# Summing the MLP's closing products in SBUF before the gate, in a four-layer diffusion trunk on one core

## The chip, the cores and the metric
The kernel runs on one core of one Trainium2 chip. The metric is the device time of one execution in microseconds; shown is the median of three runs.

## The reference, cut to what matters
Four layers (differential attention, neighbourhood attention, grouped-query attention, Hyena convolution) work on 128 context and 512 latent tokens of width 1024, all in float32. Each ends in a squared-ReLU MLP of width 4096, whose result is multiplied by a gate (one vector for the context tokens, one for the latent tokens) and added to a scaled residual before a layer norm:

```python
def squared_relu_mlp(h, w1, w2):
    return jnp.square(jax.nn.relu(h @ w1)) @ w2
...
        fp = squared_relu_mlp(modulate(xp, mod_p[3], mod_p[4]), mlp_w1[i], mlp_w2[i])
        fs = squared_relu_mlp(modulate(xs, mod_s[3], mod_s[4]), mlp_w1[i], mlp_w2[i])
        xp = layer_norm(DN_ALPHA * xp + mod_p[5] * fp, ln_g[i, 1], ln_b[i, 1])
        xs = layer_norm(DN_ALPHA * xs + mod_s[5] * fs, ln_g[i, 1], ln_b[i, 1])
```

## The kernel before, in words
The 640 tokens are five tiles of 128 (NT = 5); tile 0 is context. Every large product is made of three matmuls (mm3, L471 to L475), since each float32 operand is split into a rounded high part and a rest. Weights come in units of 512 KB: a load into one of three `raw` buffers (L421), a high part made by ACT (L450) and a rest by DVE (L451), in a fixed order of use (weight_order, L345). All loads and stores are issued by the queue of SP, in order.

The MLP (L865) goes in eight chunks of 512 of the 4096 columns. In a pass `ch` of the loop at L910 the first product of chunk `ch` is made (w1_unit, four units, L918), squared into `ff` by ACT (L875 to L877) with a rest by DVE (L878), and then the closing product of chunk `ch - 1`: 4 quarters q of 256 columns times 5 token tiles, so 20 groups of 12 matmuls, each into one of four one-bank PSUM tiles (any1). The last chunk's closing product is made by sublayer_end, beside the layer norm. The pass of ch = 0 makes only the first product.

After each group, residual (L647) empties the PSUM tile. DVE multiplies it by the gate into `gtmp` (L653), and then `gtmp` is added to the residual `r` (L660). One in four of these adds goes to DVE and three to POOL in layers 0 to 2 (`share` is QM = 1); in layer 3 all go to DVE (QL = 4). The gates come from DRAM as four tiles of 128x512, broadcast to all partitions (load_gates, L607), loaded after the pass of ch = 0; the four tiles of the layer norm's factors are loaded in the pass of ch = 6 (L917). Both sets stay until the end of the sublayer.

Between the units stands side work (side, L539). In layers 0 to 2 that is the modulation of the next layer: 48 steps, each with two 256 KB loads (`adaw`, L431) that DVE multiplies into an accumulator (L541); after every eight steps, four matmuls of PE (L546) read the accumulator. Layer 0 also makes the filter taps of the Hyena layer (L1584 to L1591), layers 1 and 2 their transforms. None of it falls into the pass of ch = 7.

Small tiles of at most 2560 bytes per partition come from one pool of general buffers, `S` (L314), NS = 16 of them: `adaw`, gates, layer-norm factors, `fx` of the MLP, the taps' tiles, and in the mixers the softmax tiles `e`, their transposes `pt`, the queries and keys.

The framework orders the instructions of each engine by a planner that follows the program's order as priority and hands out the buffers of a pool; only POOL, and PE in some stretches, keep the program's order as written. All waits are semaphores that the framework places.

Of the kernel before, what the change touches and what calls it, by code (L numbers as in the profile page):

```python
# [10 lines left out]
F32 = mybir.dt.float32  # L11
# [7 lines left out]
P = 128  # L19
D = 1024  # L20
# [4 lines left out]
NT = TOK // P  # L25
# [253 lines left out]
class Trunk:  # L279
    HL = HLN  # L280
    RAW = RAWN
    NS = 16

    def __init__(self, ctx, tc, a, outs, layers):
        self.ctx, self.tc, self.nc, self.a, self.o, self.layers = ctx, tc, tc.nc, a, outs, layers
# [28 lines left out]
    def S(self, dt, name, n=640):  # L314
        self.tn += 1
        return self.base.tile([P, n], dt, tag="S", bufs=self.NS, name=f"{name}{self.tn}")

# [491 lines left out]
    def quarter(self, u, x, t, q, quick=False):  # L809

        c = slice(t * P, (t + 1) * P)
        ps = self.any1([P, 256], "w2")
        for k in range(4):
            f = slice(k * 256, (k + 1) * 256)
            self.mm3(ps, (x[:, 0, k, c], x[:, 1, k, c]), (u[:, 0, f], u[:, 1, f]), k == 0, k == 3)
        self.residual(ps, t, q, quick)

    def out_half(self):
        self.tn += 1
# [45 lines left out]
    def mlp(self, l, nxt, last):  # L865
        nc = self.nc
        self.share = QL if last else QM
        ff = {}
        groups = 0

        def evac(dst, src):

            w = src.shape[2]
            x = self.S(F32, "fx", src.shape[1] * w).rearrange("p (a b) -> p a b", b=w)
            nc.scalar.activation(x, src, AF.Relu)  # L875
            nc.scalar.activation(x, x, AF.Square)
            nc.scalar.copy(dst[0], x)  # L877
            nc.vector.tensor_sub(dst[1], x, dst[0].bitcast(F32))  # L878

        def run(gen):  # L880
            for _ in gen:
                pass

        def w1_unit(u):
            t = self.wget(("w1", l, u))
            ps = self.b2([P, 2, 512], "w1")
            for half in range(2):
                run(self.span_a(ps[:, half, :HALF], t, half * HALF, half * HALF + HALF))
            evac([ff[u // 4][:, i, u % 4].rearrange("p (a b) -> p a b", a=2) for i in range(2)], ps[:, :, :HALF])

        def w1_first():

            ts = []
            for c0, c1 in ((0, 256), (256, TOK)):
                for pair in range(2):
                    ps = self.b2([P, 2, 512], "w1")
                    for i in range(2):
                        u = 2 * pair + i
                        if c0 == 0:
                            ts.append(self.wget(("w1", l, u), ahead=1))  # L900
                        run(self.span_a(ps[:, i, :c1 - c0], ts[u], c0, c1))
                        if c0 == 0:
                            self.flush(1)
                        else:
                            evac([ff[0][:, n, u:u + 1, c0:c1] for n in range(2)], ps[:, i:i + 1, :c1 - c0])
                    if c0 == 0:
                        evac([ff[0][:, n, 2 * pair:2 * pair + 2, c0:c1] for n in range(2)], ps[:, :, :c1 - c0])
            self.settle()

        for ch in range(8):  # L910
            ff[ch] = self.L(F32R, f"ff{ch}").rearrange("p (a f t) -> p a f t", a=2, f=4)
            if ch == 0:
                w1_first()
                self.load_gates(l, 1)
                continue
            if ch == 6:
                self.load_ln(l, 1, last)  # L917
            for f in range(4):  # L918
                w1_unit(4 * ch + f)
                self.side()  # L920
            for q in range(4):
                u = self.wget(("w2", l, 4 * (ch - 1) + q))
                for t in range(NT):
                    self.quarter(u, ff[ch - 1], t, q)
                    groups += 1
                    if self.taps and groups % TSTEP == 0:
                        self.tap_step()
                self.side()
        while self.taps:
            self.tap_step()  # L930
        self.sublayer_end(l, 1, lambda q, ahead: self.wget(("w2", l, 28 + q), ahead), lambda u, t, q, quick: self.quarter(u, ff[7], t, q, quick), last, nxt in (1, 3), nxt in (1, 2))
# [1140 lines left out]
class GqUnit(PairUnit):  # L2072
    n, chunk, cols, quick = 5, 1, FULL, 2
# [14 lines left out]
class NaUnit(PairUnit):  # L2088
    START = (0, 64, 192, 256)
    CHUNK = (1, 6, 7, 3)  # L2090
    n, quick = 3, 2
# [138 lines left out]
```

## Time and profile before

| | us |
|---|---|
| median of three runs | 3402.54 (3398.75 to 3402.73) |
| the profiled execution | 3399.52 |
| its span, first to last instruction | 3397.7 |

The profile shows one execution. Its rows give an engine's busy time (us), the number of instructions (x) and, for groups of instructions, the mean duration (ns) and how long the engine was idle just before them, with the instruction whose end released it. Windows are us from the start of the span. The four MLPs lie at about 411 to 921, 1244 to 1745, 2062 to 2555 and 2928 to 3383 us.

### The profile page before, as it was taken

What the parts mean: (1) busy time and instruction counts of PE and PEld (TensorE: products, weight loads), DVE (VectorE), ACT (ScalarE), POOL (GpSimd) and SP (SyncE); (2) the same over time, 40 slices, a digit from 0 to 9 for tenths busy, and PEclk for the clock granted to TensorE, in tenths of its full rate; (3) what the DMA queues carried; (4) which work ended last, traced back from release to release, by engine and by line L of the source; (5) the groups of instructions that cost most, each with busy time, mean ns of one, the idle gap of its engine ahead of it and who ended that gap; (6) DMA issues with size and microseconds to landing.
All of it is one profiled execution on the core that took longest, in us unless ns stands there. A gap on an engine that the chain in (4) does not pass through costs nothing.

```text
span 3397.7 us, 63734 instructions
## 1 busy us (share of the span) xinstructions
PE 3288.2 (97%) x25288; PEld 3162.0 (93%) x25288; DVE 2514.5 (74%) x4892; ACT 1526.1 (45%) x2752; POOL 677.2 (20%) x746
## 2 busy tenths in 40 slices
PE   8999999999999999999998999999998999999998
PEld 6888999998999899999997889999998998999998
DVE  4777878887766687787678888877859888855557
ACT  3667643333456564334345655333325334532322
POOL 0000123343323321222222020322321112200002
PEclk9999999999999999999999999999999999999999
DMA  8454245454343426556321123555523224322221
GB/s 285 144 156 128 72 142 178 170 167 160 94 147 103 120 69 205 174 168 211 124 78 50 32 66 117 164 175 179 175 77 126 76 97 153 106 79 75 87 75 51
DMA packets 162763, 429.45 MB, mean 126 GB/s; under 512 B 20574, under 2 KB 30438, under 8 KB 159390
## 3 DMA queue, kind: packets, MB, share of 16 engines
q1 hardware_dynamic: 162464, 425.37, 38.7%
q8 instruction: 199, 3.26, 0.4%
q14 instruction: 100, 0.82, 0.1%
HBM read 371.20 MB, written 34.05 MB: 119 GB/s over the span
## 4 chain that ended last, share of the span: by engine, by line
PE 54%; DVE 13%; issue 4%; ACT 2%; DMA 2%; POOL 2%; SPq 0%; DVEq 0%; POOLq 0%; ACTq 0%
PE w L473 13%; PE w L474 13%; PE w L475 13%; DVE hl L451 2%; PE pv L2057 1%; DVE gtmp L653 1%; DVE ada L541 1%; PE s L2010 1%; PE ptp L1060 1%; PE qk L473 1%; DMA adaw<-in_ada_w 1%; PE qk L475 1%; PE qk L474 1%; PE py L1773 1%; DVE r L660 1%
## 5 line engine op out<-in xcount | busy, mean ns | idle before, releaser
L451 DVE TENSOR_TENSOR hl<-raw,hl 128x1024 fp32r<-128x1024 f32 x411 | 535.1, 1305 | 338.1 <-ACT hl L450 336.8
L450 ACT CAST hl<-raw 128x1024 fp32r<-128x1024 f32 x411 | 430.3, 1048 | 677.0 <-PE w L475 558.8
L660 POOL TENSOR_TENSOR r<-r,gtmp 128x256 f32<-128x256 f32 x416 | 413.9, 1008 | 1564.2 <-DVE gtmp L653 1515.6
L473 PE MATMUL w<-hl,ff 128*128 128x256 f32 x2560 | 715.7, 280 | 7.3 <-DVE gtmp L653 7.0
L474 PE MATMUL w<-hl,ff 128*128 128x256 f32 x2560 | 715.2, 279 | 2.5 <-DVE hl L451 2.4
L475 PE MATMUL w<-hl,ff 128*128 128x256 f32 x2560 | 714.0, 279 | 0.0
L473 PE MATMUL w<-hh,hl 128*128 128x320 f32 (+2 forms) x2048 | 635.7, 310 | 3.8 <-ACT fx L875 3.1
L474 PE MATMUL w<-hl,hl 128*128 128x320 f32 (+2 forms) x2048 | 632.1, 309 | 3.4 <-DVE hl L742 3.3
L475 PE MATMUL w<-hh,hl 128*128 128x320 f32 (+2 forms) x2048 | 632.1, 309 | 0.0
L473 PEld LDWEIGHTS w<-hl,ff 128*128 128x128 f32 x2560 | 481.1, 188 | 11.9 <-DVE gtmp L653 10.1
L474 PEld LDWEIGHTS w<-hl,ff 128*128 128x128 f32 x2560 | 481.2, 188 | 5.0 <-DVE hl L451 3.3
L475 PEld LDWEIGHTS w<-hl,ff 128*128 128x128 f32 x2560 | 480.0, 188 | 0.0
L653 DVE TENSOR_TENSOR gtmp<-w,gate 128x256 f32<-128x256 f32 x800 | 326.6, 416 | 182.6 <-PE w L475 165.9
L541 DVE SCALAR_TENSOR_TENSOR ada<-adaw,sil,ada 128x512 f32<-128x512 f32 x504 | 388.0, 801 | 88.9 <-DMA adaw<-in_ada_w 85.4
L473 PEld LDWEIGHTS w<-hh,hl 128*128 128x128 f32 x2048 | 384.3, 188 | 18.9 <-issue 9.2
L474 PEld LDWEIGHTS w<-hl,hl 128*128 128x128 f32 x2048 | 384.2, 188 | 4.5 <-DVE hl L742 4.1
L475 PEld LDWEIGHTS w<-hh,hl 128*128 128x128 f32 x2048 | 384.1, 188 | 0.8 <-issue 0.8
L875 ACT ACTIVATE fx<-w 128x640 f32<-128x640 f32 (+2 forms) x136 | 91.5, 673 | 462.6 <-PE w L475 444.9
L473 PE MATMUL qk<-hh,hl 128*128 128x320 f32 (+2 forms) x672 | 215.1, 320 | 0.2
L474 PE MATMUL qk<-hl,hl 128*128 128x320 f32 (+2 forms) x672 | 210.6, 313 | 1.7 <-DVE hl L742 1.7
L475 PE MATMUL qk<-hh,hl 128*128 128x320 f32 (+2 forms) x672 | 210.2, 313 | 0.0
L473 PE MATMUL w<-hl,oh 128*128 128x256 f32 x640 | 183.9, 288 | 7.9 <-DVE gtmp L653 5.5
(338 smaller groups left out, 6630.6 us busy)
## 6 DMA issues: line engine op xcount, KB each, us to landing
raw<-in_w SPq DMA_DIRECT2D x256, 512.0 KB
adaw<-in_ada_w SPq DMA_DIRECT2D x288, 256.0 KB
adaw<-in_ada_w SPq DMA_DIRECT2D x16, 1024.0 KB
raw<-ab_d SPq DMA_DIRECT2D x32, 512.0 KB
raw<-in_hy_in SPq DMA_DIRECT2D x24, 512.0 KB
ks<-ks SPq DMA_DIRECT2D x64, 160.0 KB
adaw<-in_ada_s SPq DMA_DIRECT2D x8, 1024.0 KB
raw<-in_da_qk SPq DMA_DIRECT2D x16, 512.0 KB
```

Source lines behind the costliest of these rows:

```text
L450: self.nc.scalar.copy(t[:, 0], raw)
L451: self.nc.vector.tensor_sub(t[:, 1], raw, t[:, 0].bitcast(F32))
L473: mm(ps, w[0], x[0], start=start, stop=False)
L474: mm(ps, w[0], x[1], start=False, stop=False)
L475: mm(ps, w[1], x[0], start=False, stop=stop)
L541: nc.vector.scalar_tensor_tensor(out=y, in0=raw[h], scalar=x, in1=y, op0=ALU.mult, op1=ALU.add)
L653: nc.vector.tensor_mul(tmp, ps, self.gate[2 * s + q // 2][:, (q % 2) * 256:(q % 2) * 256 + 256])
L660: eng.tensor_add(rv, rv, tmp)
L875: nc.scalar.activation(x, src, AF.Relu)
L1060: nc.tensor.transpose(ps[:, i * P:(i + 1) * P], pr[:, (done + i) * P:(done + i + 1) * P], self.ident)
L1773: mm(py[ct][:, par], yh[:, i, cc], inv[h][:, kt, s, par], start=kt == 0 and i == 0 and h == 0, stop=False)
L2010: mm(ps[dst], hd["qs"][h][:, self.qs], ks[:, c], start=n == 0, stop=n == 1)
```

## The change
The closing products of chunks 0 to 5 no longer go through the gate one by one. Their 20 groups per chunk are summed in a new SBUF tile `sums` (128 x 5 x 1024, 20 KB per partition): chunk 0's groups are copied there by ACT, those of chunks 1 to 5 added by DVE, straight from PSUM. In the pass of ch = 7, beside the first product of that chunk, ten pairs of DVE instructions of 128x512 multiply `sums` by the gate and add it to `r`. Chunks 6 and 7 go as before. The gates are loaded in the pass of ch = 6 rather than after ch = 0. To make room, the general buffers go from 16 to 14 and the space kept for descriptors of software-made DMAs is cut to 1024 bytes.

```diff
-    NS = 16
+    NS = 14
...
         ps = self.any1([P, 256], "w2")
+        self.product(ps, u, x, t)
+        self.residual(ps, t, q, quick)
+
+    def product(self, ps, u, x, t):
+        c = slice(t * P, (t + 1) * P)
         for k in range(4):
             f = slice(k * 256, (k + 1) * 256)
             self.mm3(ps, (x[:, 0, k, c], x[:, 1, k, c]), (u[:, 0, f], u[:, 1, f]), k == 0, k == 3)
-        self.residual(ps, t, q, quick)
...
+        sums = self.scr.tile([P, NT, D], F32, tag="sums", bufs=1, name=f"sums{l}")
+
+        def collect(ps, t, c0, first):
+
+            v = sums[:, t, c0:c0 + ps.shape[1]]
+            if first:
+                nc.scalar.copy(v, ps)
+            else:
+                nc.vector.tensor_add(v, v, ps)
+
+        def gated(t, h):
+
+            c = slice(h * 512, (h + 1) * 512)
+            nc.vector.tensor_mul(sums[:, t, c], sums[:, t, c], self.gate[(0 if t == 0 else 2) + h])
+            nc.vector.tensor_add(self.r[:, t, c], self.r[:, t, c], sums[:, t, c])
...
             if ch == 0:
                 w1_first()
+                continue
+            if ch == 6:
                 self.load_gates(l, 1)
-                continue
             if ch == 6:
                 self.load_ln(l, 1, last)
             for f in range(4):
                 w1_unit(4 * ch + f)
+                if ch == 7:
+                    for i in range(f * 10 // 4, (f + 1) * 10 // 4):
+                        gated(i // 2, i % 2)
                 self.side()
             for q in range(4):
                 u = self.wget(("w2", l, 4 * (ch - 1) + q))
                 for t in range(NT):
-                    self.quarter(u, ff[ch - 1], t, q)
+                    if ch == 7:
+                        self.quarter(u, ff[6], t, q)
+                    else:
+                        ps = self.any1([P, 256], "w2")
+                        self.product(ps, u, ff[ch - 1], t)
+                        collect(ps, t, q * 256, ch == 1)
...
-    nc = bacc.Bacc("TRN2", target_bir_lowering=False, num_devices=1)
+    nc = bacc.Bacc("TRN2", target_bir_lowering=False, num_devices=1, dynamic_dma_scratch_size=1024)
```

## Rows read from the trace of the kernel before

**Rows 1.** The page, part 1: busy us of each engine over the span.
```profile
PE 3288.2 (97%) x25288; PEld 3162.0 (93%) x25288; DVE 2514.5 (74%) x4892; ACT 1526.1 (45%) x2752; POOL 677.2 (20%) x746
```

**Rows 2.** Windows, the four MLPs: PE, PEld, DVE, ACT, POOL busy; PEclk, DMA share, GB/s.
```profile
411.00:921.00 510.00, 496.00 (x3637) 474.20 (x3635) 401.91 (x681) 206.17 (x298) 163.36 (x159) 1.00 0.46 151
1244.00:1745.00 501.00, 496.02 (x3796) 486.64 (x3795) 378.29 (x598) 198.84 (x277) 122.47 (x118) 1.00 0.48 160
2062.00:2555.00 493.00, 488.69 (x3751) 479.89 (x3750) 371.94 (x593) 191.15 (x264) 128.08 (x118) 1.00 0.46 152
2928.00:3383.00 455.00, 453.39 (x3478) 452.27 (x3477) 261.11 (x476) 141.97 (x191) 18.89 (x14) 1.00 0.24 76
```

**Rows 3.** Waits of PE, MLP of layer 0 (411 to 921): total us, times, longest.
```profile
PE ada L546 <- DVE ada L541: 5.6, 6, 1.4
PE w L473 <- DVE gtmp L653: 3.8, 3, 1.5
PE filt L1581 <- DVE hab L1573: 2.0, 1, 2.0
...
PE ada L546 <- DVE gtmp L653: 0.2, 1, 0.2
```

**Rows 4.** Waits of PE, MLP of layer 1 (1244 to 1745).
```profile
PE w L474 <- DVE hl L451: 2.4, 2, 1.3
PE w L473 <- DVE gtmp L653: 0.9, 2, 0.6
```

**Rows 5.** Waits of PE, MLP of layer 2 (2062 to 2555).
```profile
PE w L473 <- DVE gtmp L653: 2.4, 4, 1.0
```

**Rows 6.** Groups of instructions, whole span: busy us, mean ns, idle before.
```profile
L660 POOL TENSOR_TENSOR r<-r,gtmp 128x256 f32<-128x256 f32 x416 | 413.9, 1008 | 1564.2 <-DVE gtmp L653 1515.6 <-DVE m L2015 27.4 <-DVE mv L691 15.2
L541 DVE SCALAR_TENSOR_TENSOR ada<-adaw,sil,ada 128x512 f32<-128x512 f32 x504 | 388.0, 801 | 88.9 <-DMA adaw<-in_ada_w 85.4 <-ACT ada L539 3.4
...
L653 DVE TENSOR_TENSOR gtmp<-w,gate 128x256 f32<-128x256 f32 x800 | 326.6, 416 | 182.6 <-PE w L475 165.9 <-POOL r L660 12.8 <-DMA gate<-gate_d 2.0
...
L660 DVE TENSOR_TENSOR r<-r,gtmp 128x256 f32<-128x256 f32 x364 | 167.0, 462 | 7.6
...
L749 DVE TENSOR_TENSOR r<-r,ln_b 128x512 f32<-128x512 f32 x70 | 45.6, 685 | 0.0
L748 DVE TENSOR_TENSOR r<-r,ln_g 128x512 f32<-128x512 f32 x70 | 45.5, 685 | 0.0
...
L952 ACT COPY vv<-v 128x256 f32<-128x256 f32 x40 | 14.7, 370 | 30.5 <-PE v L475 30.3
```

**Rows 7.** Tile ada, layer 0's MLP, 470 to 836: duration ns min/median/max.
```profile
L541 DVE SCALAR_TENSOR_TENSOR ada<-adaw,sil,ada x153: 730/745/1226, 471.4 to 833.6; 128x512 f32<-128x512 f32 x153
```

**Rows 8.** Timeline near 550 us, of DVE and of POOL: start us, us.
```profile
550.52 2.04 DVE L541 SCALAR_TENSOR_TENSOR ada<-adaw,sil,ada 128x512 f32<-128x512 f32 x2
...
549.67 3.49 POOL L660 TENSOR_TENSOR r<-r,gtmp 128x256 f32<-128x256 f32 x3
```

**Rows 9.** Windows, layer 0: pass ch = 6, then first product of ch = 7; neighbourhood attention.
```profile
781.00:836.00 55.00, 51.16 (x373) 46.93 (x372) 52.54 (x84) 22.07 (x31) 24.02 (x23) 1.00 0.51 176
836.00:863.00 27.00, 27.00 (x186) 27.00 (x187) 6.85 (x7) 9.31 (x13) 0.00 (x0) 1.00 0.25 79
965.00:1160.00 195.00, 194.51 (x1569) 186.13 (x1568) 114.71 (x319) 120.14 (x322) 61.49 (x136) 1.00 0.37 105
```

**Rows 10.** Groups of instructions, pass ch = 6 of layer 0 (781 to 836).
```profile
L541 DVE SCALAR_TENSOR_TENSOR ada<-adaw,sil,ada 128x512 f32<-128x512 f32 x28 | 21.6, 803 | 1.2 <-DMA adaw<-in_ada_w 1.2
```

**Rows 11.** Waits of DVE, whole span: total us, times, longest.
```profile
DVE ada L541 <- DMA adaw<-in_ada_w: 85.4, 29, 7.5
```

**Rows 12.** DMA issues, pass ch = 6 of layer 0 (781 to 836).
```profile
adaw<-in_ada_w SPq DMA_DIRECT2D x10, 256.0 KB
```

**Rows 13.** Windows, pass ch = 6 of layers 1 and 2.
```profile
1596.00:1659.00 63.00, 62.71 (x480) 60.55 (x479) 47.91 (x72) 26.48 (x34) 17.56 (x16) 1.00 0.56 194
2406.00:2468.00 62.00, 61.90 (x477) 60.10 (x476) 46.99 (x71) 26.12 (x34) 15.80 (x14) 1.00 0.55 192
```

## The prediction, made before the change was run
> **What bounds the kernel.** I read the busy times of the page first, then windows over the four MLPs, then what PE waited for in each, then the groups of instructions that the change removes or resembles. PE is busy for 3288.2 of 3397.7 us [rows 1]. In the MLPs it is busy for 496.0 of 510, 496.0 of 501, 488.7 of 493 and 453.4 of 455 us, at a granted clock of 1.00 [rows 2]. The reader is to see that the number of matmuls sets the time, and that the change leaves every matmul as it is. All that it can win in the MLPs is PE's idle time there: 14.0 + 5.0 + 4.3 + 1.6 = 24.9 us. Not all of that waits for DVE. In layer 0 PE waited 5.6 us for the accumulator of the modulation, and 3.8 and 0.2 us for a PSUM tile that DVE had yet to empty [rows 3], together 9.6; in layer 1 2.4 us for the rest of a weight and 0.9 for a PSUM tile [rows 4]; in layer 2 2.4 [rows 5]; in layer 3 nothing of the kind shows. That is 9.6 + 3.3 + 2.4 = 15.3 us, 0.45% of the time, in which DVE was late. The 2.0 us for `hab` in layer 0 hang on a load and stay.
>
> **What the change does to DVE, per MLP of layers 0 to 2.** Chunk 0: its 20 multiplies of 416 ns [rows 6] go to ACT, 8.3 us. Chunks 1 to 5: 100 multiplies become 100 adds. An add from PSUM into SBUF of that shape has no row; I take the 416 ns of the multiply, which also reads one operand of 128x256 from PSUM and one from SBUF, so 0, with 370 ns (ACT's copy of the shape) and 462 ns (DVE's add in SBUF) as ends, 4.6 us either way. The adds into `r` of chunks 0 to 5 go: 120 groups, of which DVE had 30, 30 x 0.462 = 13.9 us, and POOL 90, 90 x 1.008 = 90.7 us. The gating costs 10 x (0.685 + 0.685) = 13.7 us by the layer norm's multiply and add of 128x512 in SBUF [rows 6]. Sum: -8.3 - 13.9 + 13.7 = -8.5 us of DVE's 372 to 402 [rows 2]. In layer 3, where all 120 adds are DVE's, it is -8.3 - 55.4 + 13.7 = -50 us, worth nothing: PE has 1.6 us of idle time there.
>
> **POOL's neighbourhood.** DVE's multiply-add of the modulation takes 745 ns as a rule and up to 1226 [rows 7]; near 550 us two of them take 2.04 us while POOL adds into `r` [rows 8], where 2 x 0.745 would be 1.49. Over the span its mean is 801 [rows 6], so 504 x 0.056 = 28 us, some 9.4 per MLP. Most of it goes with POOL's adds; the taps' subtractions on POOL stay. DVE's relief is then 8.5 to 18 us per MLP. The Trainium skill, page "SBUF — State Buffer", section "Who interferes with whom", says that a DVE instruction with two SBUF inputs and a GpSimd instruction that reads SBUF exclude each other, the second one standing still until the first ends. The trace agrees on who slows whom, but shows 0.48 us for a meeting (1226 less 745), not POOL's whole 1.0 us. By the page the 90 adds could free up to 90 us of DVE per MLP, by the rows 9.4; the sum goes by the rows.
>
> **What PE gets of it.** DVE has the most to do in the pass of ch = 6 of layer 0: 52.54 of 55 us, with PE idle for 3.8 [rows 9]. The relief there is 5 adds x 0.462 + 28 multiply-adds [rows 10] x 0.056 = 3.9 us, so DVE stays over 85% busy. Elsewhere DVE is late in short bursts, where a multiply-add waits for its load: 85.4 us in 29 waits, 2.9 us each, the longest 7.5 [rows 11], all in these MLPs. These the change doesn't shorten, and what stands behind them on DVE's queue stays late. So between nothing and 15.3 us; I take half, 7.6.
>
> **What hides the new work.** ACT's 20 copies at 370 ns are 7.4 us per MLP on an engine that is busy for 40% of it [rows 2]; the cover is ACT's idle time, and the PSUM tile comes free no later than before (370 against 416 ns). If the cover is gone, the conversion of the next weights stands behind the copies, which runs two units ahead. The gating lies beside the first product of ch = 7, where DVE is busy for 6.85 of 27 us and POOL for nothing [rows 9]: 6.9 + 13.7 = 20.6 fits. At worst the three pairs behind the last unit, 4.1 us, stand ahead of the first PSUM tiles; four PSUM tiles cover that, at 1.4 us a group: layer 3's 455 us [rows 2] are eight chunks of 57, half of each 20 groups.
>
> **The gates and the buffers.** Four gate loads, 1 MB, move on SP's queue from ch = 0, past everything of ch = 1 to 5, to ch = 6, just ahead of the four layer-norm loads. At that pass's 176 GB/s [rows 9] they take 6 us, and the 10 `adaw` loads [rows 12] and the weights queue behind them. At the same place eight general buffers are held, and what is left falls from 8 to 6, while `adaw` wants 4, `fx` 1, the taps of layer 0 up to 4. In ch = 1 to 5 the number rises from 12 to 14. No row counts buffers; from below the cost is 0, as the loads run ahead, and from above one longest wait per MLP, 3 x 7.5 = 22.5 us. Nearest is the mean wait: 3 x 2.9 = 8.7 us on DVE. Of DVE's 85.4 us of such waits at most 15.3 reached PE, so 1.6 us. In the mixers 14 buffers rather than 16 hold a softmax tile or a transpose back now and then; in neighbourhood attention PE idles for only 0.5 of 195 us [rows 9], and the code lets at most about 16 be in use there, for moments. I add 1.4 us, with 0 and 10 as ends (5% of that stage). Together 3.0. The smaller descriptor space touches nothing: every load is issued by SP.
>
> **Sum.** -7.6 + 3.0 = -4.6 us. Against the profiled execution's 3399.5 that is 3394.9. That execution lies 3.0 below the median of the runs, so I predict a median of 3402.5 - 4.6 = 3398. About 0.2%, 6.8 us, is what a measurement of this kernel can tell from no change.
>
> **Rivals.** A, faster: every wait of PE for DVE goes, because DVE's queue loses both its adds and POOL as a neighbour. 15.3 us less, no cost from the buffers: 3387. For it: POOL has 90 us less per MLP, and the adds that delay PSUM tiles are gone. Against it: the waits for `adaw`. It is also what the Trainium skill's rule of exclusion (same page and section as above) would give. Chance 0.25.
>
> B, slower: the pass of ch = 6 starves for buffers. A load of `adaw` then starts only when a multiply-add has freed its tile, and DVE, which takes its instructions in order, waits for the transfer with the emptying of PSUM behind it. In layer 0 DVE has 2.5 us of idle time and 3.9 of relief, 6.4, so the third mean wait of 2.9 us reaches PE, and from the fifth the gain of 7.6 is eaten up. With eight of the ten loads late it is 8 x 2.9 - 6.4 - 7.6 = +9.2: 3412. In layers 1 and 2 DVE's 15 us of idle time in that pass [rows 13] hide as much. For it: DVE at 95%. Against it: the loads there are issued well ahead, and DVE waited only 1.2 us for `adaw` in that pass [rows 10]. Chance 0.20.
>
> C, nothing moves: PE's waits come from late transfers rather than from DVE's load, or what one group gains is lost at the next wait. 3403. For it: the waits for `adaw` [rows 11]. Chance 0.15. The forecast has 0.40.
>
> **Range and chances.** The forecast's own range is 3393 to 3404. The whole one is 3384 to 3413: A with some of the taps' waits gone as well at the lower end, B at the upper. Faster by over 0.2% is below 3395.7: A, and 0.07 of the forecast, 0.32. Slower is above 3409.3: B, 0.20. The rest, 0.48, lies within.
>
> **What would show it.** Right: `gtmp` with 320 multiplies instead of 800, an add into `sums` near 416 ns, POOL's adds into `r` fewer by about 270, the mean of L541 nearer to 745, PE's waits for DVE in layer 0 at about half of 9.6 us, layer 3's span the same. Wrong in B's way: more than 85.4 us of DVE waiting for `adaw`, in the passes of ch = 6. Wrong altogether: PE's idle time in the mixers up by over 7 us, or layer 3's MLP shorter.

## The result and the profile after

| | before | after |
|---|---|---|
| median of the runs, us | 3400.99 (3398.75 to 3402.73, 4 runs) | 3378.21 (3377.09 to 3379.34, 4 runs) |
| the profiled execution, us | 3399.52 | 3378.87 |
| its span, us | 3397.7 | 3376.8 |

The ratio is 0.9933, with a 95% interval of 0.9918 to 0.9948: 22.8 us less, where 4.6 were forecast. The time lies below the range (3384 to 3413), below rival A (3387) too.

First the page, part 1, of the kernel after (answers to [rows 1]): busy us of each engine.
```profile
PE 3278.9 (97%) x25288; PEld 3162.6 (94%) x25288; DVE 2396.6 (71%) x4682; ACT 1552.0 (46%) x2832; POOL 385.7 (11%) x476
```
The number of matmuls is the same. DVE has 118 us less to do, POOL 292 us. Next the windows over the four MLPs after (answers to [rows 2]; columns as there).
```profile
411.00:904.50 493.50, 486.80 (x3634) 473.34 (x3633) 381.30 (x648) 212.94 (x319) 77.33 (x69) 0.99 0.47 156
1229.00:1724.00 495.00, 493.38 (x3795) 486.42 (x3794) 351.81 (x567) 204.87 (x296) 23.75 (x28) 1.00 0.49 162
2045.00:2532.00 487.00, 485.32 (x3745) 478.44 (x3744) 346.20 (x560) 196.45 (x284) 23.72 (x28) 1.00 0.47 153
2907.50:3362.00 454.50, 453.01 (x3474) 452.03 (x3471) 215.95 (x354) 147.77 (x210) 18.80 (x14) 1.00 0.24 76
```
Of the 28.5 us by which the windows of layers 0 to 2 shrank, 13.3 were idle time of PE (23.3 before, 10.0 after) and 15.2 were time in which PE counted as busy (1480.7 and 1465.5). The reader is to see which stages moved. For that, each stage of both traces is taken from the first matmul of a first product to the last matmul of the eighth closing product; what lies between is a mixer. After less before, the MLPs of layers 0 to 2 are 16.3, 5.9 and 5.3 us shorter, layer 3's is 0.1 longer, and the four mixers are 6.6 longer together (-0.3, +1.3, +4.1, +1.5). That sums to -20.8 of the spans' -20.9. Over all the runs below, the first mixer lies between -2.7 and +1.7 us of before and layer 3's MLP between -0.4 and +1.1, so an entry under some 2.5 us says little.

The groups of DVE and of POOL after, and ACT's copies (answer to [rows 6]):
```profile
L541 DVE SCALAR_TENSOR_TENSOR ada<-adaw,sil,ada 128x512 f32<-128x512 f32 x504 | 358.0, 747 | 95.4 <-DMA adaw<-in_ada_w 92.6 <-ACT ada L539 2.7
L882 DVE TENSOR_TENSOR sums<-sums,w 128x256 f32<-128x256 f32 x400 | 164.1, 415 | 128.4 <-PE w L475 127.9
L653 DVE TENSOR_TENSOR gtmp<-w,gate 128x256 f32<-128x256 f32 x320 | 131.1, 417 | 79.4 <-PE w L475 71.6 <-POOL r L660 4.7 <-DMA gate<-gate_d 1.4
L887 DVE TENSOR_TENSOR sums<-sums,gate 128x512 f32<-128x512 f32 x40 | 26.6, 684 | 0.1
L888 DVE TENSOR_TENSOR r<-r,sums 128x512 f32<-128x512 f32 x40 | 26.6, 684 | 0.1
...
L880 ACT COPY sums<-w 128x256 f32<-128x256 f32 x80 | 29.8, 373 | 59.3 <-PE w L475 58.8
...
L660 POOL TENSOR_TENSOR r<-r,gtmp 128x256 f32<-128x256 f32 x146 | 120.7, 834 | 782.6 <-DVE gtmp L653 739.6 <-DVE m L2043 24.7 <-DVE mv L691 15.2
```
The prediction's prices of single instructions stand: the add from PSUM 415 ns (416 taken), ACT's copy 373 (370), the gating pair 684 each (685), L541 at 747 (745). The new work was costed rightly; what PE would get of it was not.

Where PE got it shows in a view that the prediction did not read: the waits of PEld, the weight loads. Before, the three MLPs:
```profile
PEld ada L546 <- DVE ada L541: 13.9, 11, 2.3
PEld w L473 <- DVE gtmp L653: 5.2, 4, 1.7
...
PEld w L473 <- DVE win L1585: 1.7, 2, 0.8
PEld w L474 <- DVE hl L742: 1.0, 1, 1.0
PEld ada L546 <- DVE gtmp L653: 1.0, 3, 0.4
...
PEld w L474 <- DVE hl L451: 3.3, 4, 1.5
...
PEld w L473 <- DVE gtmp L653: 1.3, 2, 0.8
...
PEld ada L546 <- DVE ada L541: 1.2, 2, 1.0
PEld w L474 <- DVE hl L742: 1.1, 1, 1.1
...
PEld w L473 <- DVE gtmp L653: 4.5, 9, 1.2
```
These are layer 0 (first five lines), layer 1 (next four) and layer 2 (the last, beside another 1.0 for `hl` L742): 22.8, 6.9 and 5.5, together 35.2 us of waiting for DVE, where PE's own rows had 15.3. After, the same view of layer 0; in layers 1 and 2 only the 1.0 for `hl` L742 is left.
```profile
PEld w L473 <- ACT fx L894: 5.7, 3, 4.4
...
PEld ada L546 <- DVE ada L541: 1.4, 2, 1.1
PEld w L474 <- DVE hl L742: 1.0, 1, 1.0
...
PEld w L473 <- DVE ab L1618: 0.8, 1, 0.8
PEld w L473 <- DVE win L1615: 0.8, 1, 0.8
PEld w L473 <- DVE win L1613: 0.8, 1, 0.8
PEld w L473 <- DVE hl L451: 0.8, 1, 0.8
PEld w L473 <- DVE win L1616: 0.8, 1, 0.8
PEld ada L546 <- DVE sums L882: 0.4, 1, 0.4
```
So 6.8, 1.0 and 1.0 us: 16.0, 5.9 and 4.5 less, near the gains of the stages (16.3, 5.9 and 5.3). The waits of 0.8 us stand behind a group of `ada` matmuls (L546) in both kernels, whichever engine they are put down to; without them layer 0 has some 20 us before and 3 after. Idle time of PEld is not PE's loss to the microsecond: in layer 0 a longer wait for ACT (5.7 us, 2.2 before) stands beside these, of which more below.

Why PE's rows hid this: the accumulator of the modulation is the operand that PEld loads, 128x32. The timeline of PE before, at one such place (start us, us):
```profile
634.20 1.50 PE L546 MATMUL ada<-ada,ones 128*32 128x512 f32 x6
636.47 1.04 PE L546 MATMUL ada<-ada,ones 128*32 128x512 f32 x2 [0.78 <-DVE ada L541]
637.45 0.41 PE L473 MATMUL w<-hh,hl 128*128 128x320 f32 x1
```
One of these matmuls lasts 605 ns by the median of its 144 records, of which the profile has eight for the four matmuls of the program. When the accumulator is there, the records overlap: at 503 us after, eight take 1.07 us together. When it is late they come mostly in twos, of 1.04 us here, and PE counts as busy while it waits for the next. From the start of each to the start of PE's next matmul, the 144 take 34.5 us before and 20.1 after; the 7680 closing products 918.8 and 901.5 by the same measure.

### The profile page after: what moved, and what is told of

Read it like the earlier page. It is cut to its first block, busy times and chain, and to the rows that moved or that the text cites. A ratio compares the mean times of both kernels' runs of the same rounds, so it can differ in the third digit from the quotient of the medians.

```text
span 3376.8 us, 63034 instructions
## 1 busy us (share of the span) xinstructions
PE 3278.9 (97%) x25288; PEld 3162.6 (94%) x25288; DVE 2396.6 (71%) x4682; ACT 1552.0 (46%) x2832; POOL 385.7 (11%) x476
## 4 chain that ended last, share of the span: by engine, by line
PE 78%; DVE 10%; issue 4%; ACT 3%; DMA 2%; POOL 2%; SPq 0%; DVEq 0%; POOLq 0%; ACTq 0%
PE w L473 18%; PE w L474 17%; PE w L475 17%; PE qk L473 3%; PE qk L474 2%; PE qk L475 2%; PE s L2038 2%; PE ptp L1088 2%; PE pv L2085 2%; PE pv L2189 1%; PE v L475 1%; PE py L1801 1%; PE v L474 1%; PE v L473 1%; DVE hl L451 1%
## 5 line engine op out<-in xcount | busy, mean ns | idle before, releaser
L451 DVE TENSOR_TENSOR hl<-raw,hl 128x1024 fp32r<-128x1024 f32 x411 | 515.9, 1256 | 395.4 <-ACT hl L450 378.2
L541 DVE SCALAR_TENSOR_TENSOR ada<-adaw,sil,ada 128x512 f32<-128x512 f32 x504 | 358.0, 747 | 95.4 <-DMA adaw<-in_ada_w 92.6
L473 PEld LDWEIGHTS w<-hh,hl 128*128 128x128 f32 x2048 | 385.1, 188 | 23.1 <-ACT fx L894 9.5
L894 ACT ACTIVATE fx<-w 128x640 f32<-128x640 f32 (+2 forms) x136 | 91.5, 672 | 465.0 <-PE w L475 448.3
L882 DVE TENSOR_TENSOR sums<-sums,w 128x256 f32<-128x256 f32 x400 | 164.1, 415 | 128.4 <-PE w L475 127.9
L660 POOL TENSOR_TENSOR r<-r,gtmp 128x256 f32<-128x256 f32 x146 | 120.7, 834 | 782.6 <-DVE gtmp L653 739.6
```

What stands on the lines that cost most here:

```text
L451: self.nc.vector.tensor_sub(t[:, 1], raw, t[:, 0].bitcast(F32))
L473: mm(ps, w[0], x[0], start=start, stop=False)
L541: nc.vector.scalar_tensor_tensor(out=y, in0=raw[h], scalar=x, in1=y, op0=ALU.mult, op1=ALU.add)
L660: eng.tensor_add(rv, rv, tmp)
L882: nc.vector.tensor_add(v, v, ps)
```

## The experiments

The question is what made DVE late before. One theory (S below) is that POOL's adds stretch the DVE instructions beside them; its rivals are that DVE waits for POOL (H: the product tiles and `r`), that DVE simply has too much to do, and that the number of free buffers in chunks 1 to 5 counts. Each kernel was run beside the one before on the same chip. Stages are as above, in us against the profiled execution of before; L546 and closing are the two start-to-next sums (34.5 and 918.8 before).

| run | median (before beside it) | ratio, 95% interval | MLP 0, 1, 2 | mixers | L546 | closing |
|---|---|---|---|---|---|---|
| after | 3378.21 (3400.99) | 0.9918 to 0.9948 | -16.3, -5.9, -5.3 | +6.6 | 20.1 | 901.5 |
| b_nopool | 3371.86 (3400.76) | 0.9901 to 0.9931 | -22.0, -5.4, -5.3 | +4.1 | 22.5 | 901.2 |
| a_pool | 3387.40 (3400.76) | 0.9949 to 0.9977 | -16.0, -0.4, -5.6 | +6.1 | 22.0 | 905.4 |
| b_gtmp | 3397.82 (3399.84) | 0.9982 to 1.0000 | -4.2, -0.9, +1.8 | +1.4 | 32.6 | 918.3 |
| b_alldve | 3389.35 (3399.84) | 0.9958 to 0.9982 | -5.2, +0.4, -6.8 | +2.4 | 35.7 | 901.5 |
| b_pooltiny | 3374.53 (3400.64) | 0.9909 to 0.9939 | -17.9, -5.7, -6.1 | +4.0 | 26.9 | 900.9 |
| b_poolfree | 3396.56 (3400.64) | 0.9983 to 1.0002 | -13.7, +3.5, +2.2 | +0.9 | 28.1 | 918.8 |
| b_nodveadd | 3383.31 (3400.64) | 0.9933 to 0.9967 | -13.5, -3.0, -0.4 | +2.1 | 26.9 | 912.5 |
| b_ns14 | 3408.08 (3400.76) | 1.0011 to 1.0029 | +2.5, -1.3, +1.2 | +7.8 | 33.6 | 920.2 |
| a_gates0 | 3372.53 (3400.76) | 0.9905 to 0.9934 | -25.1, -5.9, -5.4 | +9.5 | 20.0 | 901.1 |
| a_ln7 | 3373.81 (3399.84) | 0.9910 to 0.9937 | -23.1, -6.4, -6.2 | +4.6 | 19.9 | 901.8 |
| a_dve0 | 3376.29 (3399.84) | 0.9916 to 0.9943 | -18.0, -6.1, -6.0 | +9.5 | 20.0 | 900.0 |
| a_mix16 | 3369.87 (3400.64) | 0.9897 to 0.9926 | -20.8, -5.9, -5.1 | +1.3 | 21.3 | 901.6 |

### Which part carries the gain

**b_nopool**: before, without POOL's 270 adds of chunks 0 to 5 of layers 0 to 2.
```diff
+        if skip and eng is nc.gpsimd:
+            return
...
-                    self.quarter(u, ff[ch - 1], t, q)
+                    self.quarter(u, ff[ch - 1], t, q, skip=ch < 7)
```
Expected:

> The kernel before, with POOL's adds into r of chunks 0 to 5 in layers 0 to 2 left out (270 of 416; the sum lacks them), DVE's multiplies and its own adds as before. POOL theory (the MLPs gain because POOL no longer slows DVE and no longer holds the three gtmp tiles): the MLPs of layers 0 to 2 are 20 us or more shorter, 3380 us in all. Own-load theory (they gain because DVE itself has fewer and shorter instructions): under 8 us shorter, 3393 us or more.

Measured 3371.86: the gates' place, the multiplies, DVE's own adds and the 16 buffers are as before, and the whole gain of the MLPs is there (-32.7 against -27.5 after). Taking POOL's adds away is enough for it.

**a_pool**: after, with POOL given back adds of the same size, on data that nobody waits for.
```diff
                 nc.vector.tensor_add(v, v, ps)
+            self.rt = (self.rt + 1) % 4
+            if self.rt >= self.share:
+                tmp = self.base.tile([P, 256], F32, tag="gtmp", bufs=3, name=f"gtmp_x{self.tn}_{t}_{c0}")
+                nc.gpsimd.tensor_add(tmp, self.r[:, t, c0:c0 + 256], self.r[:, t, c0:c0 + 256])
```
Expected:

> The kernel after, with three adds of POOL for every four summed groups put back in layers 0 to 2: each adds a piece of r to itself into a gtmp tile that nobody reads, so that POOL is as busy as before but nothing waits for it except the next user of the gtmp tile. POOL theory, by way of the shared port: 15 us or more of the MLPs' 27.5 come back, and the mean of the modulation's multiply-add goes from 747 ns back to about 800. By way of the gtmp tiles, or own-load theory: under 6 us come back, although the mean of the multiply-add rises.

Measured 3387.40, 9.2 us above after (5.8 by the profiled executions). L541's mean rises to 797 ns again, yet MLP0 keeps its gain, and MLP1 loses 5.5, with a single stall of 4.0 us at 1301.7; the 15 us that one theory gave did not come back. So POOL beside DVE costs something, but not as much as before: DVE has none of its own adds here, and nobody waits for POOL. In layers 1 and 2 POOL's adds also lie otherwise than before. As they wait for nobody they run in two blocks of 43 and 45 without a gap, 37 to 47 us long, where the kernel before has at most four in a row. In layer 0 they are spread over the chunks, nearly as before.

**b_gtmp** and **b_alldve**: before with twelve product tiles, and before with all adds on DVE.
```diff
-        tmp = self.base.tile([P, 256], F32, tag="gtmp", bufs=3, name=f"gtmp{self.tn}")
+        tmp = self.base.tile([P, 256], F32, tag="gtmp", bufs=12, name=f"gtmp{self.tn}")
```
```diff
-        self.share = QL if last else QM
+        self.share = QL
```
Expected of b_gtmp:

> The kernel before with 12 gtmp tiles instead of 3 (and the smaller descriptor space, which makes the room), 16 general buffers, every multiply and add as before. Leaving out POOL's adds gave the MLPs 32.7 us; putting POOL's work back on a tile that nobody reads took little of the change's gain, although the multiply-add slowed to 797 ns. Tile theory (DVE's multiply, and with it the emptying of PSUM, stood still until POOL's add had freed one of three gtmp tiles): the MLPs of layers 0 to 2 are 20 us or more shorter, the mixers unchanged, 3380 us or less. If POOL's adds cost by their order on r or by the port instead: under 8 us.

Expected of b_alldve:

> The kernel before with all adds into r of the MLPs on DVE, none on POOL. Tile theory: nothing waits for POOL any more, but DVE has 90 x 0.462 = 41.6 us more in the first six chunks of each MLP of layers 0 to 2 (480 adds' share in all of them). Where DVE is 95% busy (pass of ch = 6 of layer 0) it must become the bound; with POOL gone and DVE loaded the MLP of layer 0 is longer than before by 5 us or more, those of layers 1 and 2 (DVE at 75%) shorter by 3 to 5. Own-load theory: all three longer.

By DVE's waits in MLP0 before, it stood 8.9 us for POOL to give a product tile back. With twelve tiles (and the smaller descriptor space, to make room) no such wait is left, and that brings 4.2 us there and nothing elsewhere: the three tiles are not the main cause. With all adds on DVE the closing products run as fast as after (901.5) though DVE has 270 adds more in chunks 0 to 5, while the modulation's matmuls are as late as before (35.7). None of the cases named for b_alldve came: MLP0 is shorter instead of longer, and why MLP1 gains nothing (+0.4) while MLP2 gains 6.8 was not traced.

**b_pooltiny, b_poolfree, b_nodveadd**: three runs to part the handshake from the neighbourhood. In the first POOL's adds keep their dependences but take 8 of 256 columns; in the second (with the smaller descriptor space) they keep their size but write a tile that nobody reads; in the third DVE's 90 adds go and POOL's stay.
```diff
+        if skip and eng is nc.gpsimd:
+            eng.tensor_add(rv[:, :8], rv[:, :8], tmp[:, :8])
+            return
```
```diff
+        if skip and eng is nc.gpsimd:
+            own = self.base.tile([P, 256], F32, tag="own", bufs=3, name=f"own{self.tn}")
+            eng.tensor_add(own, rv, rv)
+            return
```
```diff
+        if skip and eng is nc.vector:
+            return
```
Expected of b_pooltiny:

> The kernel before, with the 270 POOL adds of chunks 0 to 5 kept in place with their dependences on gtmp and r, but over 8 of the 256 columns (the other 248 columns of these sums are left out). Theory S: L541 falls to about 747 ns, as where the adds are left out, and 3374 us (3370 to 3380). Theory H: the handshakes are as many as before, and 3395 us (3388 to 3402), with DVE waits for POOL r of several us left in MLP0.

Expected of b_poolfree:

> The kernel before, with the 270 POOL adds of chunks 0 to 5 kept as instructions of the same size, but each adds r to itself into a tile of its own that nobody reads: POOL is as busy beside DVE as before, and nobody on DVE waits for it. The sums are therefore left out, as in b_nopool. Theory S (POOL beside DVE stretches DVE's instructions that read two operands from SBUF, and DVE, near full in MLP0, falls behind): L541 stays at about 800 ns, the closing products' start-to-next time at about 915 us, 3396 us (3390 to 3402). Theory H (DVE waits for POOL's handshake on gtmp or r): the gain of b_nopool comes, 3373 us (3368 to 3378). A time in between, near 3385, splits it.

Expected of b_nodveadd:

> The kernel before, with the 90 DVE adds of chunks 0 to 5 of layers 0 to 2 left out (a quarter of the sums), POOL's kept. They take 14.7 us of DVE in MLP0. If DVE near full is what counts, whoever fills it, MLP0 wins 12 to 16 us although POOL runs as before (as a_pool had it), and the whole 16 to 22: 3383 us (3378 to 3387). If it is POOL alone that holds things up, under 5 us: 3397 us.

The times came out where theory S, and DVE near full for the third, had them: 3374.53, 3396.56, 3383.31. For b_poolfree that is in part luck, as its stages show. In MLP0, where its adds are spread nearly as before, it wins 13.7 of b_nopool's 22.0 us although the columns are all there, and L541 is at 784 ns (801 before), not at 800. In layers 1 and 2 its adds run in gapless blocks of 43 and 45, as in a_pool, and stalls behind the first blocks take the gain away; so it says little of these layers as they were before.

The firmer run is b_pooltiny. With the handshakes kept and the columns taken away, layers 1 and 2 have the whole gain and MLP0 17.9 of 22.0 us. Its adds end sooner as well, after 551 ns where they took 1008 on average, so that a handshake is also shorter: in the windows below DVE waits 8.0 us for POOL to free a product tile before, and 4.8 in b_pooltiny. In layers 1 and 2 such waits were only 1.1 and 1.6 us, and b_gtmp, without them, won nothing clear there; that leaves the stretch as the likely reason. In MLP0 stretch and wait are not parted.

The view that shows the stretch is DVE's work in the same part of MLP0, from the first closing products to the first product of chunk 7. Before, the window and DVE's largest groups:
```profile
483.50:875.00 391.50, 379.19 (x2748) 358.64 (x2747) 309.03 (x505) 149.26 (x205) 139.66 (x134) 1.00 0.49 161
...
L541 DVE SCALAR_TENSOR_TENSOR ada<-adaw,sil,ada 128x512 f32<-128x512 f32 x147 | 112.7, 799 | 15.8 <-DMA adaw<-in_ada_w 15.8
L451 DVE TENSOR_TENSOR hl<-raw,hl 128x1024 fp32r<-128x1024 f32 x50 | 67.0, 1339 | 38.3 <-ACT hl L450 38.3
```
b_pooltiny, its groups taken over 482 to 857 us:
```profile
483.00:859.00 376.00, 372.47 (x2749) 356.53 (x2749) 292.61 (x504) 149.20 (x205) 90.18 (x134) 1.00 0.51 167
...
L541 DVE SCALAR_TENSOR_TENSOR ada<-adaw,sil,ada 128x512 f32<-128x512 f32 x148 | 105.8, 748 | 17.1 <-DMA adaw<-in_ada_w 17.1
L451 DVE TENSOR_TENSOR hl<-raw,hl 128x1024 fp32r<-128x1024 f32 x49 | 60.7, 1239 | 41.6 <-ACT hl L450 41.6
```
The same instructions take DVE 309.0 us in one and 292.6 in the other. The prediction had counted L541 alone (9.4 us per MLP); the rests of the weights, L451, are stretched as well, by 100 ns each. POOL's instructions are as many in both (134 in the window), so it is their size that counts, not their number.

In layer 1 b_poolfree shows the stretch undiluted, since its adds, which wait for nobody, run one after the other. Its timeline of POOL, then of DVE (start us, us):
```profile
1279.74 20.41 POOL L659 TENSOR_TENSOR own<-r 128x256 f32<-128x256 f32 x18
...
1285.00 4.16 DVE L541 SCALAR_TENSOR_TENSOR ada<-adaw,sil,ada 128x512 f32<-128x512 f32 x4
1289.08 1.63 DVE L451 TENSOR_TENSOR hl<-raw,hl 128x1024 fp32r<-128x1024 f32 x1
1290.63 1.23 DVE L882 TENSOR_TENSOR ff<-fx,ff 128x640 fp32r<-128x640 f32 x1
```
The timeline before, first POOL and DVE at a place in MLP0, then the same three forms of DVE without POOL beside them:
```profile
693.39 3.27 POOL L660 TENSOR_TENSOR r<-r,gtmp 128x256 f32<-128x256 f32 x3
...
693.64 1.76 DVE L451 TENSOR_TENSOR hl<-raw,hl 128x1024 fp32r<-128x1024 f32 x1
...
695.92 0.41 DVE L653 TENSOR_TENSOR gtmp<-w,gate 128x256 f32<-128x256 f32 x1
...
1298.48 2.73 DVE L541 SCALAR_TENSOR_TENSOR ada<-adaw,sil,ada 128x512 f32<-128x512 f32 x4
1301.13 1.22 DVE L451 TENSOR_TENSOR hl<-raw,hl 128x1024 fp32r<-128x1024 f32 x1
...
1302.97 0.82 DVE L878 TENSOR_TENSOR ff<-fx,ff 128x640 fp32r<-128x640 f32 x1
```
Four of L541 go from 2.73 to 4.16 us, L451 from 1.22 to 1.63, the rest of `ff` from 0.82 to 1.23: each instruction is 0.36 to 0.41 us longer here, whatever its length. POOL's adds last 1.06 us beside L541 there, 1.59 beside L451 and 1.19 beside the rest of `ff`: one add to each DVE instruction, as if the two took turns. Elsewhere the price varies: L451 at 693.64 takes 1.76 us, 0.54 more than alone, and six of L541 in the second block of layer 1 (1431 to 1468 us) run at 0.76 or 0.77. The multiply of a PSUM tile by the gate is not stretched: 0.41 us at 695.92 while POOL adds, and its mean is 412 and 414 ns in the two windows above (L653, 121 and 119 instructions). PE's stall of 4.7 us at 1297.5 comes behind this stretch, and behind a wait of DVE of 5.8 us for a load of `adaw` (2.7 us between 1265 and 1310 before). One more of 4.8 follows in layer 2. With them layers 1 and 2 are 3.5 and 2.2 us longer than before, where b_nopool has them 5.4 and 5.3 shorter. a_pool's stall at 1301.7 stands in the first block of its adds, which began at 1256 us.

MLP0 is less clean: there the handshakes alone cost something (b_poolfree -13.7), DVE's own adds do (b_nodveadd -13.5), the columns most (b_pooltiny -17.9), and these do not add up to b_nopool's -22.0. What they share is DVE's lateness. From the start of a group's last matmul to the start of the instruction that empties its PSUM tile it is 2.8 us on average in chunks 0 to 5 of MLP0 before and up to 6.6, near the 5.7 us of work that four PSUM tiles hold; 2.4 in b_nodveadd, 2.1 in b_poolfree, 1.6 in b_pooltiny, 1.4 in b_nopool, and 1.5 after in chunks 1 to 5 (3.0 before there). b_alldve stands apart, at 2.0 with only 5.2 us won: its modulation is still late. How much of MLP0's gain is the stretch, the handshake and DVE's own load stays open; that taking POOL's adds away brings the whole of it is what b_nopool shows.

### Which part takes some of it back

**b_ns14**: before with 14 general buffers and the smaller descriptor space.
```diff
-    NS = 16
+    NS = 14
```
Expected:

> The kernel before with 14 general buffers instead of 16 and the smaller descriptor space, nothing else. After the change the four MLPs together are 27.5 us shorter and the mixers together 6.6 us longer (grouped-query attention 4.1, the others about 1.4 each). If the longer mixers come from the two buffers, they are 5 to 8 us longer here too; if from something else (the order of instructions carried over from the MLPs), under 2. Buffer theory (the MLPs gain because 14 instead of 12 buffers are free in the passes of ch = 1 to 5): the MLPs are longer here by 10 us or more, as 10 are free. The other theories: MLPs within 3 us of before, except the pass of ch = 6 in layer 0.

Measured 3408.08, 7.3 us slower. Over all runs, grouped-query attention (the mixer of layer 2) is 3.4 to 5.3 us longer in the six with 14 buffers and -0.6 to +0.7 in the seven others, Hyena 1.4 to 2.4 against 0.0 to 1.3; the first two mixers don't tell the two apart. The descriptor space is not the reason, since b_gtmp, b_poolfree and a_mix16 have a smaller one with 16 buffers. One of PE's waits that differ there, the one for a softmax tile, after, then in a_mix16 (16 buffers); the rest of the 4 us was not traced:
```profile
PE s L2038 <- ACT e L2112: 3.1, 4, 2.0
```
```profile
PE s L2037 <- ACT e L2111: 1.7, 6, 0.5
```

**a_gates0, a_ln7, a_dve0**: after, with the gates loaded after chunk 0 as before; with the layer norm's factors in ch = 7; with chunk 0's copies on DVE.
```diff
                 w1_first()
+                self.load_gates(l, 1)
                 continue
-            if ch == 6:
-                self.load_gates(l, 1)
```
```diff
-            if ch == 6:
+            if ch == 7:
                 self.load_ln(l, 1, last)
```
```diff
-                nc.scalar.copy(v, ps)
+                nc.vector.tensor_copy(v, ps)
```
Expected of a_gates0:

> The kernel after with the gates loaded after the pass of ch = 0, as before, so that 10 general buffers are free in the passes of ch = 1 to 5 instead of 14. Buffer theory: the MLPs of layers 0 to 2 are 10 us or more longer than after the change. The other theories: within 3 us, and PE's single wait of 4.2 us in the pass of ch = 6 of layer 0 shrinks, if the four gate loads (1 MB) ahead of the layer-norm loads caused it; it stays if eight held buffers did.

Expected of a_ln7:

> The kernel after with the layer norm's four factor tiles loaded in the pass of ch = 7 instead of 6; the gates still in ch = 6. Loading the gates early gave 6.9 us back in the pass of ch = 5 to 6 of layer 0. If what cost them is the burst of 2 MB of broadcast loads ahead of the adaw loads, or eight held buffers, half of either gives most of it back here too: MLP of layer 0 shorter than after by 4 us or more. If it is the gate loads alone (their place in the order), nothing changes there.

Expected of a_dve0:

> The kernel after with chunk 0's 20 copies made by DVE instead of ACT. Own-load theory: 20 x 0.37 to 0.42 = 8 us more on DVE in the pass of ch = 1, which in layer 0 gained 5.2 us; most of that is given back. Tile theory: under 1.5 us, as nothing there waits for POOL in either case.

With the gates back after chunk 0, four buffers fewer are free in chunks 1 to 5, and MLP0 is 8.8 us shorter than after, not longer; moving the other set away brings 6.8. So the two sets collide. The waits after at the start of the pass of ch = 6 (755 to 785 us), two rows of ACT's timeline and windows there:
```profile
DVE ada L541 <- DMA adaw<-in_ada_w: 9.5, 1, 9.5
...
ACT ln_g L795 <- DMA ln_g<-in_ln_g: 5.6, 2, 3.3
...
PE w L473 <- ACT fx L894: 4.2, 1, 4.2
...
764.98 0.63 ACT L795 ACTIVATE ln_b<-ln_b 128x512 f32<-128x512 f32 x1 [0.81 <-DMA ln_b<-in_ln_b]
765.52 0.69 ACT L894 ACTIVATE fx<-w 128x640 f32<-128x640 f32 x1
...
761.00:767.00 6.00, 1.83 (x11) 1.57 (x10) 0.09 (x1) 2.87 (x5) 0.00 (x0) 0.82 0.92 312
767.00:771.00 4.00, 4.00 (x17) 4.00 (x17) 3.90 (x6) 3.78 (x5) 0.00 (x0) 0.50 0.44 142
771.00:775.00 4.00, 4.00 (x27) 4.00 (x27) 4.00 (x6) 0.00 (x0) 0.00 (x0) 0.92 0.75 218
```
ACT scales the layer norm's factors (L795) ahead of `fx` (L894), the instruction that empties the PSUM tile PE waits for. Their loads stand behind those of the gates, and ACT waits for them 6.9 us in all; `fx` starts as the last scaling ends, and PE, which stood 4.2 us, goes on at 766.26. Before, ACT stood for these loads as well, but this `fx` began 15.0 us after the first matmul of the pass, where it is 18.2 here, and PE waited at most 0.7 us for it. DVE stands 9.5 us before a load of `adaw` in the same stretch, but only until 766.91, after PE has gone on: that wait is not what held PE. Then the granted clock is 0.50, 1.2 GHz, up to 771.5 us: 20 matmuls start 0.267 us apart instead of 0.147, another 2.4 us. In a_gates0 `fx` starts at 759.70, ahead of the last scaling; no wait of PE shows in that stretch and PE is busy for 30.00 of 30 us. Who makes chunk 0's copies does not show (a_dve0: 0.2 to 1.7 us per MLP, within what such stages vary by).

**a_mix16**: after with the gates after chunk 0, `sums` for four of the five token tiles, the fifth gated as before with its adds on DVE, and 16 buffers (512 bytes for the descriptors).
```diff
-        sums = self.scr.tile([P, NT, D], F32, tag="sums", bufs=1, name=f"sums{l}")
+        sums = self.scr.tile([P, NT - 1, D], F32, tag="sums", bufs=1, name=f"sums{l}")
...
-                    if ch == 7:
-                        self.quarter(u, ff[6], t, q)
+                    if ch == 7 or t == NT - 1:
+                        self.quarter(u, ff[ch - 1], t, q, quick=ch < 7)
```
Expected:

> A version meant to beat both: the kernel after with its gates loaded after chunk 0 (a_gates0, 3372.5), the sums kept for four of the five token tiles alone, the fifth gated product by product as before with its adds on DVE, which leaves room for 16 general buffers. If the 14 buffers are what the mixers lose 6 to 8 us by, the mixers stand within 2 us of before and the MLPs within 3 us of a_gates0: 3367 us (3363 to 3371). If 24 more DVE adds a layer make MLP0 late again as in b_alldve, MLP0 loses 8 us or more against a_gates0: 3375 us. If the mixers' loss comes from elsewhere, they stay 6 us or more above before: 3373 us.

Measured 3369.87, the fastest of all: the mixers are back (+1.3), MLP0 is 4.3 us behind a_gates0, between the two cases given. Its interval and that of after overlap a little (0.9926 and 0.9918), so that it beats after is likely rather than shown; against before both are clear.

## Why the prediction was wrong

**The bound.** "All that it can win in the MLPs is PE's idle time there", 24.9 us, and of that 15.3 for DVE. This step failed. The MLPs won 27.5 us, and in the windows of layers 0 to 2 some 15.2 us of what went was time in which PE counted as busy. An operand can be late at PEld while PE counts as busy; PEld's own waits for DVE in the windows of [rows 3 to 5] were 35.2 us, and 8.8 of them are left.

**"So between nothing and 15.3 us; I take half, 7.6."** That is the mis-sized term. Of the 15.3 us themselves 15.1 went: a wait of 0.2 us for the accumulator in layer 0 is all that is left of those rows, so on this point rival A was right. With the busy time the term measured 27.5 for the three MLPs, and 36 with the collision of the loads taken away (a_gates0, a_ln7). The reason for halving was that the waits for `adaw` stay and with them PE's. DVE's waits for `adaw` did stay (85.4 us before, 92.6 after), but PE's waits for DVE went all the same. What held it up in MLP0 was a backlog of 2.8 us on average that POOL's adds and DVE's own kept up.

**POOL's neighbourhood.** The mechanism was right, its size too small: 9.4 us per MLP were counted from L541 alone, where DVE's time in MLP0 differs by 16.4 between before and b_pooltiny. The Trainium skill's rule of exclusion (page "SBUF — State Buffer", section "Who interferes with whom") would have given more, up to 90 us per MLP by the prediction's estimate, and spoke for rival A. The trace agrees with the direction and not with a stop for the whole of an instruction. In the stretch of b_poolfree one L541 and one POOL add are done every 1.02 us. Four of L541 without POOL start 0.66 us apart, and a POOL add lasts 0.74 us by the median of the 416 before; one after the other they would take 1.40.

**The buffers.** 1.4 us for the mixers measured 7.8 in b_ns14 and 6.6 after, two thirds of it in one stage. The reasoning looked at neighbourhood attention, which moves as much with 16 buffers (-0.6 to +2.8) as with 14; the stage that did change, grouped-query attention, was not looked at. The end of 10 us held.

**The gates in ch = 6.** 1.6 us measured 7 to 9 in MLP0. The place was right, and the path was another. The prediction and rival B followed the loads of `adaw` to DVE; one wait of 9.5 us did come there, only in layer 0, but PE's 4.2 us came by way of ACT, which scales the layer norm's factors: as a path to PE that stood in no term. Nor did the matmuls at half the clock behind that wait. B had the sign of this part right and was outweighed.

**The rest held:** the prices of the new instructions, layer 3 unchanged, ACT's copies hidden, and the gating hidden beside ch = 7: the stretch that holds it is 3.2 us shorter in layer 0.

## What to carry to other kernels

Ask for the waits of the weight loads as well as of the matmuls before a bound is taken from PE's idle time: in the profile a late operand of short matmuls counts as busy. Work given to POOL beside DVE is priced by all of DVE's two-SBUF-operand instructions that it meets, and by what then waits behind them; it is not free because POOL has time. Where a change moves loads, look at what is loaded at the new place already and at every engine that waits for it, and where it takes buffers, at every stage that shares the pool. A run that keeps an instruction but cuts its waits may move the instruction: look where it went before reading the time.

## What the runs showed of the hardware

- Beside POOL adds from SBUF that follow one another without a gap (b_poolfree, 1285 to 1292 us) a DVE instruction with two SBUF operands was 0.36 to 0.41 us longer, for 128x512, 128x640 and 128x1024 alike, and one POOL add ended for each of them. In the other places named above it was between nothing and 0.54 us. With one operand in PSUM it was not longer (412 and 414 ns). POOL's adds over 8 columns, 551 ns each, did not stretch L541 (748 ns).
- Up to a wait of PE of 4.2 us the matmuls ran at a granted clock of 1.00; behind it they ran at 0.50 for some 5 us. A stall of 4.7 us in b_poolfree was followed by 0.59 over 4 us.
- Matmuls with a 128x32 operand last 605 ns each, but overlap when they follow one another: eight took 1.07 us.
